# Modulation weights in hh and hl, small loads on GpSimd's queue, and an earlier place for casts of w_out, in a two-layer decoder trunk

## The chip, the cores and the metric

The kernel runs on one core of a Trainium2 chip. The metric is the device time of one execution in microseconds; several executions are timed and their median is given. One execution is also recorded by the hardware profiler; its rows are what the text reads.

## The reference

Two layers work on x of 512 positions by 1024 features, all in float32. Each layer has a token-mixing half and a feed-forward half, both modulated by a vector c:

```python
for l in range(DEPTH):                                     # 2
    mod = c_act @ ada_w[l] + ada_b[l]                      # 1024 -> 6 x 1024
    shift1, scale1, gate1, shift2, scale2, gate2 = jnp.split(mod, N_MOD, axis=-1)
    h = _modulate(x, shift1, scale1)                       # x * (1 + scale) + shift
    proj = jnp.einsum('bsd,de->bse', h, w_in[l])           # a | u | v, 3 x 512
    y_a = _pool_mixer(a, pool_w[l], pool_scale[l])         # trailing means, 4 groups
    y_b = _sgu_mixer(u, v, ...)                            # gelu(u) * (tril(W) Norm(gelu(v)) + b)
    f = jnp.einsum('bse,ed->bsd', jnp.concatenate([y_a, y_b], -1), w_out[l])
    x = _layernorm(DEEPNORM_ALPHA * x + gate1[:, None, :] * f, ln1_g[l], ln1_b[l])
    h = _modulate(x, shift2, scale2)
    g, val = split(jnp.einsum('bsd,df->bsf', h, w_up[l]))  # 2 x 2816
    f = jnp.einsum('bsf,fd->bsd', jax.nn.gelu(_causal_dwconv(g, ...)) * val, w_down[l])
    x = _layernorm(DEEPNORM_ALPHA * x + gate2[:, None, :] * f, ln2_g[l], ln2_b[l])
```

## The kernel before

Every weight comes from HBM in tiles of 128 x 1024 floats (512 KB), and each product is done in three parts: a weight is split into whi (a cast on ScalarE, L156) and wlo (a subtraction on VectorE, L159, the *low part*), an activation into hh and hl, mh and ml or gh and gl, and hi by hi, hi by lo and lo by hi are added on TensorE. Loads go through four raw tiles; split weights through six pairs.

The modulation (mod above) is not a product on TensorE: for each of the 6 x 8 pieces of a layer a 512 KB tile of ada_w is loaded and VectorE multiplies it with c and sums along the row (ada_sum, L206, a *modulation sum* of 128 x 1024). Tiles for these weights are three of their own (ada) and the four tiles xr, into which x itself is loaded later: when an xr tile has been summed and at least X_AT = 14 loads have been made, the next load into it is x (L213). For layer 0, pieces 1 and 0 (scale1, shift1) are summed first, two per step; then pieces 2, 4 and 3, 24 sums that pump() strews over the rest of the mixing half, in numbers that MIX_FILL and OUT_FILL fix. gate1 (piece 2) is needed by the first residual (L292), scale2 and shift2 (pieces 4, 3) by the modulation behind the norm.

Everything is written in one order, each engine works through its instructions in that order, and so does SP, which issues all loads. Layer 0 begins with a loop of eight steps k (L495): in each, two modulation sums give scale and shift for 128 features, ScalarE makes hh[k] and then x modulated in float32 (L475, L476), VectorE makes hl[k] (L479), and TensorE adds the products of step k to a and v (L527, L530), which lie in eight PSUM banks. Loads for step k + 2 are issued in step k. The order of w_in is in FIRST. Behind that loop SP loads what is small: pool_w, sgu_w and sgu_b (256 KB each), the counts of the trailing means (rcnt), columns of layer 1 (cols) and, as single floats, the gain and bias of the gating norm (sgc, sbc).

Then come u's four products (u_tile), the pooling on VectorE (pool_group), the norm of v, z (z_mms on TensorE, z_mix: two VectorE instructions per head, a cast mh on ScalarE, and ml on VectorE), the output projection by w_out: first half of the columns for all four chunks of 128 positions (project), then the second half chunk by chunk (project_and_norm). In the latter VectorE makes the residual and the norm of a chunk, and TensorE transposes it (tr_n, L302), one chunk behind its products. Each refill(1) splits one more weight: cast, low part, and a load that takes the raw tile which came free.

Of the kernel before, what the change touches and what calls it, by code (L numbers as in the profile page):

```python
# [29 lines left out]
X_AT = 14  # L30
# [9 lines left out]
def trunk(ctx: ExitStack, tc: tile.TileContext, a: dict, out: bass.AP):  # L40
# [6 lines left out]
    wsplit = ctx.enter_context(tc.tile_pool(name="wsplit", bufs=N_SPLIT))  # L47
    rows = ctx.enter_context(tc.tile_pool(name="rows", bufs=2))
# [23 lines left out]
    ada_free = araw + xr  # L72

    def load_ada(at):
        raw = ada_free.pop(0)
        nc.sync.dma_start(raw, a["ada_w"][at])
        return raw

# [118 lines left out]


# [16 lines left out]
    def ada_load(n):  # L215
        for _ in range(n):
            i = ada_at["load"]
            if i < len(ada):
                ada_raw.append(load_ada(ada[i]))
                ada_at["load"] += 1  # L220
# [10 lines left out]
    def pump(n=1, upto=None):  # L231

        for _ in range(n):
# [3 lines left out]
            ada_load(len(ada_free) - 1)  # L237
# [29 lines left out]
    hh = const.tile([P, KD, S], F32R, name="hh")  # L267
    hl = const.tile([P, KD, S], F32R, name="hl")
# [187 lines left out]
    def first_load(k):  # L456

        if k >= KD:
            ada_load(k - KD + 2)
# [4 lines left out]
        wload(len(FIRST[k]))  # L464
# [28 lines left out]
    first_lo(0)  # L493
    late.pop()()
    for k in range(KD):  # L495
# [10 lines left out]
        if k + 1 < KD:  # L506
            first_w(k + 1, late)
            first_h(k + 1, *firsts[k + 1])
            for f in late:
                f()  # L510
            late.clear()
            first_lo(k + 1)
# [37 lines left out]
    for l in range(L):  # L550
# [8 lines left out]
        poolw, wst, sb = [unit(f"{n}{l}") for n in ("poolw", "wst", "sb")]  # L559
        nc.sync.dma_start(poolw, a["pool_w"][l])  # L560
        nc.sync.dma_start(wst, a["sgu_w"][l])
        nc.sync.dma_start(sb, a["sgu_b"][l : l + 1, :].partition_broadcast(P))
        if l == 0:
            nc.sync.dma_start(rcnt, a["rcnt"])
            nc.sync.dma_start(cols[1], a["cols"][1])
            with nc.allow_non_contiguous_dma(reason="columns of the gating norm"):
                for t, n in ((sgc, "sgu_ln_g"), (sbc, "sgu_ln_b")):
                    for i in range(L):
                        nc.sync.dma_start(t[:, i, :], a[n][i].rearrange("(h d) -> d h", h=4))
# [137 lines left out]
        else:  # L707
# [22 lines left out]
            ps = u_tile(3)  # L730
            step(pms)
# [22 lines left out]
        ada_flush(True)  # L754
        AB = affine_cols(l, 1, col[:, C_G1 : C_G1 + 8], col[:, C_B1 : C_B1 + 8])
# [127 lines left out]
```

## Time and profile before

| what | value |
|---|---|
| median of 3 runs | 1022.68 us (1021.92 to 1022.88) |
| the profiled execution, time | 1023.64 us |
| the profiled execution, span | 1021.9 us |
| TensorE (PE) busy | 986.9 us, 97% |
| VectorE (DVE) busy | 650.2 us, 64% |
| ScalarE (ACT) busy | 364.0 us, 36% |

A busy share is a mean over the whole span. The change touches the first 140 us of it, where the engines are loaded otherwise than later; what waits there is read from timelines (instructions in order of time, with the idle time ahead of each and what ended it), from the sums of waits, and from windows that give the work of each engine in a stretch.

### The profile page before, as it was taken

The numbers are of one execution on the slowest core, as the hardware profiler recorded it, in microseconds if no ns is written. First come the engines' busy times: TensorE is split into PE (matmuls) and PEld (weight loads), VectorE is DVE, ScalarE is ACT, GpSimd is POOL, SyncE is SP. The second block draws the span as 40 slices with busy tenths as digits, with TensorE's granted clock in tenths as the row PEclk, the third lists the DMA queues.
The fourth block names the chain that finished last, engine by engine and source line by source line (L and its number), as shares of the span: only waits on it lengthen the run. The fifth ranks groups of instructions, "written<-read, shape, count | busy, mean of one in ns | idle before, by whom it ended". The sixth has DMA issues, their size and how long they took to land.

```text
span 1021.9 us, 12000 instructions
## 1 busy us (share of the span) xinstructions
PE 986.9 (97%) x4691; PEld 826.8 (81%) x4691; DVE 650.2 (64%) x907; ACT 364.0 (36%) x532; POOL 102.6 (10%) x80
## 2 busy tenths in 40 slices
PE   7999778999999999999999999999999999999996
PEld 6888568888888888888889878888888888888886
DVE  7878786878754276585599554877544245544456
ACT  4553254434322233333263432733433123333300
POOL 0020017200000000000045100450000000000002
PEclk9999999999999999999999999999999999999999
DMA  9985714666642355467114321345323322323302
GB/s 355 406 305 182 249 44 168 233 217 226 207 142 83 124 172 199 143 230 247 61 62 162 106 73 42 104 168 203 113 94 104 103 86 100 103 83 103 124 1 83
DMA packets 46233, 153.55 MB, mean 150 GB/s; under 512 B 7264, under 2 KB 7520, under 8 KB 46176
## 3 DMA queue, kind: packets, MB, share of 16 engines
q1 hardware_dynamic: 46176, 152.78, 43.7%
q8 instruction: 37, 0.61, 0.3%
q14 instruction: 20, 0.16, 0.0%
HBM read 150.67 MB, written 2.10 MB: 149 GB/s over the span
## 4 chain that ended last, share of the span: by engine, by line
PE 85%; DVE 9%; DMA 2%; ACT 1%; issue 1%; POOL 1%; SPq 0%; DVEq 0%; POOLq 0%; ACTq 0%
PE up L195 15%; PE up L196 15%; PE up L194 15%; PE down L342 6%; PE down L341 6%; PE down L340 6%; PE v L527 2%; PE u L196 1%; PE u L195 1%; PE u L194 1%; DVE wlo L159 1%; DVE res L292 1%; PE a L527 1%; DVE stn L381 1%; DMA ada<-in_ada_w_dram 1%
## 5 line engine op out<-in xcount | busy, mean ns | idle before, releaser
L196 PE MATMUL up<-hh,wlo 128*128 128x512 f32 (+1 forms) x768 | 286.1, 373 | 2.4 <-DVE wlo L159 2.4
L195 PE MATMUL up<-hl,whi 128*128 128x512 f32 (+1 forms) x768 | 286.0, 372 | 2.3 <-DVE hl L317 2.3
L194 PE MATMUL up<-hh,whi 128*128 128x512 f32 (+1 forms) x768 | 286.5, 373 | 0.0
L159 DVE TENSOR_TENSOR wlo<-raw_w_up,whi 128x1024 fp32r<-128x1024 f32 x88 | 119.0, 1357 | 143.4 <-ACT whi L156 143.4
L195 PEld LDWEIGHTS up<-hl,whi 128*128 128x128 f32 x768 | 145.4, 189 | 27.7 <-DVE hl L317 2.7
L196 PEld LDWEIGHTS up<-hh,wlo 128*128 128x128 f32 x768 | 145.3, 189 | 27.5 <-DVE wlo L159 2.8
L194 PEld LDWEIGHTS up<-hh,whi 128*128 128x128 f32 x768 | 145.4, 189 | 24.9
L159 DVE TENSOR_TENSOR wlo<-raw_w_down,whi 128x1024 fp32r<-128x1024 f32 x44 | 53.9, 1225 | 114.9 <-ACT whi L156 114.9
L156 ACT CAST whi<-raw_w_up 128x1024 fp32r<-128x1024 f32 x88 | 90.9, 1045 | 57.0 <-PE down L342 52.6
L340 PE MATMUL down<-whi,gh 128*128 128x512 f32 x272 | 105.8, 389 | 0.0
L341 PE MATMUL down<-wlo,gh 128*128 128x512 f32 x272 | 105.8, 389 | 0.0
L342 PE MATMUL down<-whi,gl 128*128 128x512 f32 x272 | 105.8, 389 | 0.0
L206 DVE SCALAR_TENSOR_TENSOR ada<-ada,c 128x1024 f32<-128x1024 f32 x80 | 97.2, 1219 | 8.7 <-DMA ada<-in_ada_w_dram 8.5
L777 ACT ACTIVATE y<-y 128x512 f32<-128x512 f32 x44 | 27.9, 634 | 143.2 <-DVE y L774 143.2
L156 ACT CAST whi<-raw_w_down 128x1024 fp32r<-128x1024 f32 x44 | 46.1, 1047 | 80.6 <-PE down L342 76.2
L767 ACT ACTIVATE y<-up,cols 128x512 f32<-128x512 f32 x44 | 34.3, 780 | 90.9 <-PE up L196 90.9
L341 PEld LDWEIGHTS down<-wlo,gh 128*128 128x128 f32 x272 | 51.1, 188 | 10.7
L340 PEld LDWEIGHTS down<-whi,gh 128*128 128x128 f32 x272 | 51.1, 188 | 10.6
L342 PEld LDWEIGHTS down<-whi,gl 128*128 128x128 f32 x272 | 51.0, 188 | 10.5
L314 ACT ACTIVATE ht_n<-tr_n,B,A 128x128 f32<-128x128 f32 x96 | 36.1, 455 | 64.5 <-PE tr_n L302 64.5
L275 POOL TENSOR_SCALAR rs_n<-mv_n 128x1 f32<-128x1 f32 x12 | 7.2, 600 | 490.6 <-DVE mv_n L273 490.6
L781 ACT CAST gh<-y 128x512 fp32r<-128x512 f32 x44 | 27.3, 621 | 43.7 <-DVE y L779 43.7
(159 smaller groups left out, 1449.4 us busy)
## 6 DMA issues: line engine op xcount, KB each, us to landing
raw_w_up<-in_w_up_dram SPq DMA_DIRECT2D x88, 512.0 KB, 3.3
ada<-in_ada_w_dram SPq DMA_DIRECT2D x80, 512.0 KB, 4.4
raw_w_down<-in_w_down_dram SPq DMA_DIRECT2D x44, 512.0 KB, 3.3
raw_w_in<-in_w_in_dram SPq DMA_DIRECT2D x24, 512.0 KB, 5.7
xr<-in_ada_w_dram SPq DMA_DIRECT2D x16, 512.0 KB, 9.2
raw_w_out<-in_w_out_dram SPq DMA_DIRECT2D x16, 512.0 KB, 4.2
xT<-in_xT_dram SPq DMA_DIRECT2D x8, 256.0 KB, 9.0
xr<-in_x_dram SPq DMA_DIRECT2D x4, 512.0 KB, 4.4
```

The costliest lines, as they stand in the source:

```text
L156: A.copy(hi, src)
L159: (eng or V).tensor_tensor(lo, src, hi.bitcast(F32), op=ALU.subtract)
L194: T.matmul(ps, w[0], x[0], start=start, stop=False)
L195: T.matmul(ps, w[0], x[1], start=False, stop=False)
L196: T.matmul(ps, w[1], x[0], start=False, stop=stop)
L206: V.scalar_tensor_tensor(raw, raw, 0.5, c2, op0=ALU.mult, op1=ALU.mult, accum_out=modc[l][:, o : o + 1])
L314: A.activation(tmp[:, w], ps[hf][:, w], AF.Identity, bias=cb[:, k : k + 1], scale=ca[:, k : k + 1])
L340: T.matmul(ps[:, f], ah[:, cs], wh, start=i + j == 0, stop=False)
L341: T.matmul(ps[:, f], ah[:, cs], wl, start=False, stop=False)
L342: T.matmul(ps[:, f], al[:, cs], wh, start=False, stop=i + j == n - 1)
L527: T.matmul(ps, x, y, start=k == 0 and i == 0, stop=False)
L767: A.activation(y, pg, AF.Identity, bias=col[:, C_CB + j : C_CB + j + 1], scale=col[:, cw + 2 : cw + 3])
```

## The change

- hh and hl are no longer fixed tiles. A pool of four tiles of 128 x 4 x 512 (tag h) holds them; a small class, Parts, gives slices by step as before. When u's last product is written, hand_over() issues all four loads of x into xr, and takes the four pool tiles as eight tiles for modulation weights (lent_h). After the first half of the output projection hh and hl are taken from the pool again.
- Two tiles of the rows of the norms (tag nrow), not yet in use, are lent to the modulation weights from the beginning (lent). Loads from the 12th of the list on (LENT = 11) take only tiles of their own until hand_over(); after it, loads up to the 24th take any.
- The small loads are issued on GpSimd's queue at the beginning.
- The first w_in load stands ahead of the second ada_w load; in step 0 the products of v come ahead of those of a.
- hl[k] is written on VectorE after the first modulation sum of the next step.
- The casts of the third and fourth w_out tile stand ahead of the z casts, with their low parts later, and two modulation sums stand ahead of the second w_out's low part.

```diff
-X_AT = 14
+LENT = 11
...
+    hpool = ctx.enter_context(tc.tile_pool(name="hpool", bufs=4))
...
-    ada_free = araw + xr
+    lent = xr + [rows.tile([P, D], F32, tag="nrow", name=f"lent{i}") for i in range(2)]
+    ada_free = araw + lent
...
+    class Parts:
+        def renew(self, name):
+            self.tiles = [hpool.tile([P, 4, S], F32R, tag="h", name=f"{name}{i}") for i in range(2)]
...
+    poolw, wst, sb = mix_loads(0, G)
+    G.dma_start(rcnt, a["rcnt"])
+    G.dma_start(cols[1], a["cols"][1])
+    with nc.allow_non_contiguous_dma(reason="columns of the gating norm"):
+        for t, n in ((sgc, "sgu_ln_g"), (sbc, "sgu_ln_b")):
+            for i in range(L):
+                G.dma_start(t[:, i, :], a[n][i].rearrange("(h d) -> d h", h=4))
...
-        c = next((c for c in range(NCH) if xr[c] is raw), None)
-        if c is None or ada_at["load"] < X_AT:
-            ada_free.append(raw)
-        else:
-            nc.sync.dma_start(raw, a["x"][c * P : (c + 1) * P, :])
+        ada_free.append(raw)
...
+            own = i >= (24 if mixed else LENT)
...
+    def hand_over():
+        for c in range(NCH):
+            nc.sync.dma_start(xr[c], a["x"][c * P : (c + 1) * P, :])
+        mixed.append(True)
+        ada_free[:] = [t for t in ada_free if among(t, araw)]
+        for i in range(4):
+            t = hpool.tile([P, 4, S], F32, tag="h", name=f"lent_h{i}").rearrange("p a b -> p (a b)")
+            ada_free.extend([t[:, :D], t[:, D:]])
...
-        raw = [load_ada((0, v, k)) for v in (1, 0)]
+        raw = [load_ada((0, 1, k))]
+        wload(k == 0)
+        raw.append(load_ada((0, 0, k)))
...
             ada_sum(0, 1 - v, k, raw[v])
+            if k and v == 0:
+                first_lo(k - 1)
...
+        if k == 0:
+            products = products[1:] + products[:1]
...
             ps = u_tile(3)
+            hand_over()
             step(pms)
             pump(MIX_FILL[2], fill)
             pms = step([pool_mix(2), pool_mix(3)])
             u_gelu(3, ps)
-            refill(1)
-            step(pms)
+            refill(1, None, late)
             z_mms()
             pump(MIX_FILL[3], fill)
+            late.pop()()
+            step(pms)
+            refill(1, None, late)
             zs = step([z_mix(0), z_mix(1)])
-            refill(1)
+            late.pop()()
             pump(MIX_FILL[4], fill)
             step(zs)
+            refill(1, None, late)
             zs = step([z_mix(2), z_mix(3)])
-            refill(1)
+            late.pop()()
...
+        if l == 0:
+            hh.renew("hh")
+            hl.renew("hl")
```

Where it moves instructions is seen best in the engines' own lists. On SP, at the start, before: ada_78 and ada_79 are modulation weights, raw_w_in the first two tiles of w_in.

```order
L76 DMA ada_78<-in_ada_w_dram 128x1024
L76 DMA ada_79<-in_ada_w_dram 128x1024
L463 DMA xT_158<-in_xT_dram 128x512
L66 DMA raw_w_in_160<-in_w_in_dram 128x1024
L66 DMA raw_w_in_162<-in_w_in_dram 128x1024
```

The same place now:

```order
L82 DMA ada_81<-in_ada_w_dram 128x1024
L67 DMA raw_w_in_176<-in_w_in_dram 128x1024
L82 DMA ada_82<-in_ada_w_dram 128x1024
L512 DMA xT_179<-in_xT_dram 128x512
L67 DMA raw_w_in_181<-in_w_in_dram 128x1024
```

The first tile of w_in moved from the fourth place to the second. Further down on SP, around the loads of x, before (raw_w_out are the tiles of w_out in their order):

```order
L213 DMA xr_81<-in_x_dram 128x1024
L66 DMA raw_w_out_642<-in_w_out_dram 128x1024
L66 DMA raw_w_out_690<-in_w_out_dram 128x1024
L66 DMA raw_w_out_764<-in_w_out_dram 128x1024
L213 DMA xr_82<-in_x_dram 128x1024
L213 DMA xr_83<-in_x_dram 128x1024
L66 DMA raw_w_out_813<-in_w_out_dram 128x1024
L213 DMA xr_84<-in_x_dram 128x1024
L66 DMA raw_w_out_856<-in_w_out_dram 128x1024
L76 DMA ada_80<-in_ada_w_dram 128x1024
L66 DMA raw_w_out_878<-in_w_out_dram 128x1024
L76 DMA ada_78<-in_ada_w_dram 128x1024
```

And now, from the third tile of w_out on:

```order
L67 DMA raw_w_out_769<-in_w_out_dram 128x1024
L264 DMA xr_84<-in_x_dram 128x1024
L264 DMA xr_85<-in_x_dram 128x1024
L264 DMA xr_86<-in_x_dram 128x1024
L264 DMA xr_87<-in_x_dram 128x1024
L82 DMA ada_83<-in_ada_w_dram 128x1024
L82 DMA lent_h_801<-in_ada_w_dram 128x1024 x2
...
L67 DMA raw_w_out_832<-in_w_out_dram 128x1024
L82 DMA lent_88<-in_ada_w_dram 128x1024
L82 DMA lent_89<-in_ada_w_dram 128x1024
L67 DMA raw_w_out_864<-in_w_out_dram 128x1024
```

The loads of x stand together, and eight loads into hh and hl (lent_h, of which two are shown) stand ahead of the fourth tile of w_out. On VectorE, behind the low parts of the first two poolings' outputs, before (L206 is a modulation sum, L159 a low part of w_out, L602 and L649 are ml, L637 and L645 z):

```order
L206 SCALAR_TENSOR_TENSOR xr_83,modc_146<-xr_83,c_102 128x1024
L159 TENSOR_TENSOR wlo_810<-raw_w_out_690,whi_809 128x1024
L602 SCALAR_TENSOR_TENSOR ml_801<-pm_798,psc_537,mh_800 128x512
L602 SCALAR_TENSOR_TENSOR ml_806<-pm_803,psc_537,mh_805 128x512
L206 SCALAR_TENSOR_TENSOR xr_84,modc_146<-xr_84,c_102 128x1024
L206 SCALAR_TENSOR_TENSOR ada_78,modc_146<-ada_78,c_102 128x1024
L637 SCALAR_TENSOR_TENSOR z_840<-z_817,sgc,zb_542 128x512
L645 TENSOR_TENSOR z_840<-z_840,u_610 128x512
L637 SCALAR_TENSOR_TENSOR z_846<-z_822,sgc,zb_542 128x512
L645 TENSOR_TENSOR z_846<-z_846,u_669 128x512
L159 TENSOR_TENSOR wlo_853<-raw_w_out_764,whi_852 128x1024
```

And now:

```order
L243 SCALAR_TENSOR_TENSOR lent_89,modc_155<-lent_89,c_111 128x1024
L243 SCALAR_TENSOR_TENSOR ada_81,modc_155<-ada_81,c_111 128x1024
L243 SCALAR_TENSOR_TENSOR ada_82,modc_155<-ada_82,c_111 128x1024
L181 TENSOR_TENSOR wlo_830<-raw_w_out_695,whi_829 128x1024
L646 SCALAR_TENSOR_TENSOR ml_821<-pm_818,psc_547,mh_820 128x512
L646 SCALAR_TENSOR_TENSOR ml_826<-pm_823,psc_547,mh_825 128x512
L681 SCALAR_TENSOR_TENSOR z_866<-z_834,sgc,zb_552 128x512
L689 TENSOR_TENSOR z_866<-z_866,u_619 128x512
L681 SCALAR_TENSOR_TENSOR z_872<-z_839,sgc,zb_552 128x512
L689 TENSOR_TENSOR z_872<-z_872,u_674 128x512
L181 TENSOR_TENSOR wlo_862<-raw_w_out_769,whi_861 128x1024
```

Two sums moved from behind the second w_out's low part to ahead of it; the rest stands as it did.

## Rows read from the trace of the kernel before

**Rows 1.** TensorE's timeline: start us, us, instruction, [idle before <- what ended it].
```profile
12.71 0.80 PE L527 MATMUL a<-hh,whi 128*128 128x512 f32 x1 [3.67 <-ACT whi L156]
24.50 0.39 PE L196 MATMUL a<-hh,wlo 128*128 128x512 f32 x1
84.72 1.88 PE L597 MATMUL pm<-ws,poolw 128*128 128x512 f32 x4
136.27 1.07 PE L302 MATMUL tr_n<-ident,xr 128*128 128x128 f32 x8 [3.62 <-DVE xr L387]
```

**Rows 2.** Waits in the first 200 us: who waits for whom, total us, times, longest.
```profile
PE n_pj L341 <- DVE wlo L159: 5.4, 2, 4.0
PE out L342 <- DVE ml L649: 1.2, 1, 1.2
PE out L341 <- DVE wlo L159: 0.5, 1, 0.5
DVE ada L206 <- DMA ada<-in_ada_w_dram: 8.5, 5, 4.1
```

**Rows 3.** VectorE's timeline, same columns as rows 1.
```profile
21.23 2.36 DVE L159 TENSOR_TENSOR wlo<-raw_w_in,whi 128x1024 fp32r<-128x1024 f32 x2
59.11 1.22 DVE L206 SCALAR_TENSOR_TENSOR ada<-ada,c 128x1024 f32<-128x1024 f32 x1 [4.13 <-DMA ada<-in_ada_w_dram]
69.58 1.23 DVE L159 TENSOR_TENSOR wlo<-raw_w_in,whi 128x1024 fp32r<-128x1024 f32 x1 [1.63 <-ACT whi L156]
84.45 1.22 DVE L206 SCALAR_TENSOR_TENSOR xr<-xr,c 128x1024 f32<-128x1024 f32 x1
85.59 1.22 DVE L206 SCALAR_TENSOR_TENSOR xr<-xr,c 128x1024 f32<-128x1024 f32 x1
88.77 1.23 DVE L159 TENSOR_TENSOR wlo<-raw_w_out,whi 128x1024 fp32r<-128x1024 f32 x1 [1.96 <-ACT whi L156]
93.52 0.75 DVE L637 SCALAR_TENSOR_TENSOR z<-z,sgc,zb 128x512 f32<-128x512 f32 x1
98.02 1.23 DVE L159 TENSOR_TENSOR wlo<-raw_w_out,whi 128x1024 fp32r<-128x1024 f32 x1 [1.64 <-ACT whi L156]
106.01 1.22 DVE L159 TENSOR_TENSOR wlo<-raw_w_out,whi 128x1024 fp32r<-128x1024 f32 x1 [1.63 <-ACT whi L156]
109.50 1.22 DVE L159 TENSOR_TENSOR wlo<-raw_w_out,whi 128x1024 fp32r<-128x1024 f32 x1
128.22 1.23 DVE L206 SCALAR_TENSOR_TENSOR ada<-ada,c 128x1024 f32<-128x1024 f32 x1 [1.30 <-DMA ada<-in_ada_w_dram]
130.13 0.68 DVE L292 TENSOR_TENSOR res<-out,gate 128x512 f32<-128x512 f32 x1
```

**Rows 4.** Windows: stretch, busy us by engine, granted clock, DMA share, GB/s last.
```profile
44.00:53.00 9.00, 9.00 (x41) 7.48 (x40) 8.48 (x21) 2.78 (x4) 0.00 (x0) 1.00 1.03 404
53.00:55.50 2.50, 2.50 (x12) 2.07 (x12) 1.98 (x4) 0.00 (x0) 0.64 (x1) 1.00 0.65 95
76.00:86.00 10.00, 10.00 (x43) 7.17 (x42) 9.76 (x21) 4.10 (x7) 0.00 (x0) 1.00 0.02 7
```

**Rows 5.** SP's timeline of issues: start us, us, line, loads in a row.
```profile
68.40 2.77 SPq L66 DMA_DIRECT2D raw_w_out<-in_w_out_dram  x3
85.70 1.47 SPq L213 DMA_DIRECT2D xr<-in_x_dram  x2
```

**Rows 6.** Loads by tile: count, KB each, median us from issue to landing.
```profile
raw_w_up<-in_w_up_dram SPq DMA_DIRECT2D x88, 512.0 KB, 3.3
poolw<-in_pool_w_dram SPq DMA_DIRECT2D x2, 256.0 KB, 6.9
```

**Rows 7.** ScalarE's timeline, same columns as rows 1.
```profile
10.07 0.81 ACT L475 ACTIVATE hh<-xT,B,A 128x512 fp32r<-128x512 f32 x1
20.69 1.05 ACT L156 CAST whi<-raw_w_in 128x1024 fp32r<-128x1024 f32 x1 [0.23 <-DMA raw_w_in<-in_w_in_dram]
87.70 1.04 ACT L156 CAST whi<-raw_w_out 128x1024 fp32r<-128x1024 f32 x1
```

More of the change, by code (lines that the diff above doesn't have):

```diff
@@ L71, in trunk, with among, load_ada, __getitem__ @@
     xr = [const.tile([P, D], F32, name=f"xr{c}") for c in range(NCH)]
-    ada_free = araw + xr
-    def load_ada(at):
-        raw = ada_free.pop(0)
+    lent = xr + [rows.tile([P, D], F32, tag="nrow", name=f"lent{i}") for i in range(2)]
+    ada_free = araw + lent
+    def among(t, ts):
+        return any(t is x for x in ts)
+    def load_ada(at, own=False):
+        raw = next(t for t in ada_free if not own or among(t, araw))
+        ada_free[:] = [t for t in ada_free if t is not raw]
         nc.sync.dma_start(raw, a["ada_w"][at])
         return raw
+    class Parts:
+        def renew(self, name):
+            self.tiles = [hpool.tile([P, 4, S], F32R, tag="h", name=f"{name}{i}") for i in range(2)]
+        def __getitem__(self, at):
+            _, k, t = at
+            if isinstance(k, slice):
+                return self.tiles[k.start // 4][:, :, t]
+            return self.tiles[k // 4][:, k % 4, t]
+    hh, hl = Parts(), Parts()
+    hh.renew("hh_0")
+    hl.renew("hl_0")
     c_in = const.tile([P, KD], F32, name="c_in")
@@ L196, in mm3, with mix_loads @@
         T.matmul(ps, w[1], x[0], start=False, stop=stop)
+    def mix_loads(l, eng):
+        tiles = [unit(f"{n}{l}") for n in ("poolw", "wst", "sb")]
+        eng.dma_start(tiles[0], a["pool_w"][l])
+        eng.dma_start(tiles[1], a["sgu_w"][l])
+        eng.dma_start(tiles[2], a["sgu_b"][l : l + 1, :].partition_broadcast(P))
+        return tiles
+    poolw, wst, sb = mix_loads(0, G)
[5 more added lines that the diff above has]
+                G.dma_start(t[:, i, :], a[n][i].rearrange("(h d) -> d h", h=4))
     ada = [(0, v) for v in (2, 4, 3, 5)] + [(1, v) for v in (1, 0, 2, 4, 3, 5)]
@@ L208, in ada_sum, with ada_load @@
         )
-        c = next((c for c in range(NCH) if xr[c] is raw), None)
-        if c is None or ada_at["load"] < X_AT:
-            ada_free.append(raw)
-        else:
-            nc.sync.dma_start(raw, a["x"][c * P : (c + 1) * P, :])
-    def ada_load(n):
-        for _ in range(n):
-            i = ada_at["load"]
-            if i < len(ada):
-                ada_raw.append(load_ada(ada[i]))
-                ada_at["load"] += 1
+        ada_free.append(raw)
+    def ada_load(keep=0, most=9):
+        for _ in range(most):
+            i = ada_at["load"]
+            own = i >= (24 if mixed else LENT)
+            if i >= len(ada) or sum(1 for t in ada_free if not own or among(t, araw)) <= keep:
+                return
+            ada_raw.append(load_ada(ada[i], own))
+            ada_at["load"] += 1
+    mixed = []
+    def hand_over():
[6 more added lines that the diff above has]
+            ada_free.extend([t[:, :D], t[:, D:]])
     def ada_flush(now=False):
@@ L236, in pump @@
                 return
-            ada_load(len(ada_free) - 1)
+            ada_load(1)
             l, v, n_ = ada[i]
@@ L265, in affine_cols @@
         return ca, cb
-    hh = const.tile([P, KD, S], F32R, name="hh")
-    hl = const.tile([P, KD, S], F32R, name="hl")
     def rstd_of(st, name):
@@ L458, in first_load @@
         if k >= KD:
-            ada_load(k - KD + 2)
+            ada_load(1, 4)
             return
-        raw = [load_ada((0, v, k)) for v in (1, 0)]
+        raw = [load_ada((0, 1, k))]
+        wload(k == 0)
+        raw.append(load_ada((0, 0, k)))
         x = unit(f"xT{k}")
         nc.sync.dma_start(x, a["xT"][k])
-        wload(len(FIRST[k]))
+        wload(len(FIRST[k]) - (k == 0))
         firsts.append((x, raw))
@@ L492, in trunk @@
     refill(1, None, late)
-    first_lo(0)
     late.pop()()
@@ L511, in trunk @@
             late.clear()
-            first_lo(k + 1)
+        else:
+            first_lo(k)
         for ps, w in zip(a_ps[old:], a_w[old:]):
@@ L558, in trunk @@
             next_residuals(grow2, brow2)
[L559 to L569, printed above, removed]
+        if l:
+            poolw, wst, sb = mix_loads(l, nc.sync)
         at = []
```

## The prediction

> **What bounds the kernel now.** Read first where TensorE stands still [rows 1, 2]: it is the busy engine of this kernel, so a change pays where it waits. That is in three places: ahead of its first product (12.71 us), between 106 and 136 us (the three groups of waits for w_out's low parts and for ml in rows 2, and 3.62 us ahead of the first transposition, at 136.27), and for a little after that. Everything in the second place names VectorE. So the next view is VectorE's timeline [rows 3]: from 84 to 130 us it is almost full, and at its end stands the step that matters, the first residual at 130.13, which needs the gate and comes behind the 24 modulation sums of this layer in VectorE's order. From there to the transposition that TensorE waits for are 6.14 us (130.13 to 136.27), a chain of VectorE and GpSimd. So the end of this stretch is set by when VectorE gets through its list, and the question is how much of the list's time is waiting. Rows 2 and 3 tell: 1.96, 1.64 and 1.63 us for ScalarE's casts of w_out at 88.77, 98.02 and 106.01, and 8.5 us in five waits for modulation weights from HBM; the longest, 4.13 us, ends at 59.11, and the other four, 4.4 us, come late, the last at 128.22. The last view is the DMA's: in 76 to 86 us it moves 7 GB/s, while a full stretch moves 404 [rows 4]. The reason is SP's queue [rows 5]: after the third w_out load, at 71 us, its next entry, a load of x into an xr tile, waits until 85.70 for VectorE to have summed what is in that tile, and all weights stand behind it.
>
> **Edit 1: the tiles and SP's order.** Two tiles more (nine for seven) hold modulation weights, and when u is done eight more lie in hh and hl. SP's order puts all four loads of x and one of modulation weights right behind the third w_out load, then the eight lent loads, which wait for TensorE's last products of u. Those end at 84.72 [rows 1], and a load takes 3.3 us to land [rows 6], so the lent loads land from about 88 us on at 1.30 us each (512 KB at 404 GB/s), the eighth by 98. Behind them stand the fourth w_out load (99 to 100) and the last two of the 24 sums' loads (102 to 103). The new wait on SP is thus the one for u, with everything down to w_up queued behind it; the queue stands empty meanwhile, as it did before. Who needs it: the sums 15 to 24, the first at about 102 us and the last at 118 (below), so the margin is over 10 us; the fourth w_out, cast at about 100 and wanted by VectorE at 100.6, which is the tight one, at most a few tenths; and w_out five to eight, landed by about 110 and wanted from 104 to 116. The four DMA waits of 4.4 us go.
>
> **Edit 2: casts ahead of z's, two sums earlier.** On ScalarE the third w_out cast moves ahead of the first two z casts, the fourth ahead of the next two; none waits for z any more, and ScalarE has time there (the second cast is at 87.70 [rows 7], the first z at 93.52). On VectorE two sums move ahead of the second w_out's low part, into the 1.96 us wait. I walk the new list with the pitch of rows 3: a sum 1.14 us (84.45 to 85.59), a low part the same (its row, as the sum's, says 1.22, of which 0.08 overlap the next), a z 1.4 (two from 93.52 to 96.38, where the wait of 1.64 begins), a pair of ml 1.2 to 1.3. The start is 84.45 as before: up to 69.58 VectorE now runs ahead of ScalarE, but there it waits for a cast that stands behind ScalarE's norm and gelu, whose order is unchanged, and from 69.58 to 84.45 it is full either way. So what VectorE saves before 69.58 (the 4.13 us wait among it) is **not** gained. From 84.45: four sums to 89.0, low part to 90.2, two ml to 91.5, two z to 94.3, low part 95.4, sum 96.6, two ml 97.8, two z 100.6, low part 101.7, sum 102.9, two ml 104.1; then four low parts, nine sums and the columns of the affine, 4.6 + 10.3 + 0.8, to 119.8. Before it was 130.13: **10.3 us less**. From below: the waits named are 1.96 + 1.64 + 1.63 + 4.4 = 9.6; from above, the list without any gap, 10.6.
>
> Is VectorE still the last one then? TensorE was done with the second chunk's products at 136.27 - 3.62 = 132.65; less its waits for low parts and ml, 0.5 + 1.2 + 5.4 [rows 2], it would be by 125.5; the transposition's data come at 119.8 + 6.1 = 125.9. They are nearly equal, so more than 0.4 us beyond this could not be had on VectorE alone. Behind that point the orders of all engines are the same in both kernels, and so are the waits up to the first up-projection (SP's loads of the norm's rows behind w_up, ScalarE behind those): they move with it. hh and hl are taken again after the last sum that reads a lent tile, which is over by then: no wait.
>
> **Edit 3: the start.** The first w_in load moves one place up, and the first products use it alone (v ahead of a): they need its cast and hh, which ends at 10.07 + 0.81 = 10.9 [rows 7], so TensorE starts up to 1.8 us before 12.71. But this is not kept. The third step's weights are the next fence: the cast at 20.69 waits for their landing [rows 7], the two low parts run from 21.23 to 23.6 [rows 3], and TensorE takes the second at 24.50 [rows 1]. So at most 0.9 us is gained. hl one sum later costs nothing: VectorE gives up waits of half a us for ScalarE there, and TensorE reads hl only at the end of each step.
>
> **Edit 4: small loads on GpSimd's queue.** They leave SP's queue and now run at the very start. Price: three loads of 256 KB [rows 6] and 0.1 MB besides, 0.89 MB at 404 GB/s, 2.2 us; and four loads of single floats (512 pieces each): in 53 to 55.5 us [rows 4], where they ran before, the DMA was busy 0.65 of 2.5 us, 1.6, while its 0.24 MB are worth 0.6, so 1.0 us. In the first 50 us HBM's stream is the fence, so landings come 2.2 to 3.2 us later: the cast of the third step ends at 21.7 + 2.2 to 3.2, its low part 1.14 later, 25.0 to 26.0 against 24.50, a loss of 0.5 to 1.5 us. Later steps have more slack (TensorE does 8 groups a step by then), so it stays at that. No row shows a DMA from GpSimd, so the term lies between a gain of 0.9 (they come later than the third step) and 1.5 lost; I take **0.8 lost**, since the stretch at 404 GB/s leaves nothing free. TensorE, ScalarE's norms and so VectorE's 69.58 all move with it. The Trainium skill, page "DMA: Bandwidth & Descriptors", section "Queues, rings and completion order", says that a DMA engine takes turns between the rings that have work, packet by packet; no run here shows it with a GpSimd queue, and it would put the small loads into the first 10 us rather than behind SP's stream.
>
> **Sum.** -10.3 + 0.8 = -9.5. The profiled execution took 1023.64 us (span 1021.9), 1 us over the median; it would become 1014.1, and the median of 1022.68 becomes **1013.2**. The bounds: 1022.68 - 10.6 - 0.9 = 1011.2 to 1022.68 - 9.6 + 1.5 = 1014.6.
>
> **Rivals.**
> (a) The small loads come late and the start's 0.9 us is kept: 1022.68 - 10.3 - 0.9 = 1011.5. For it: GpSimd has to make these transfers itself, one after the other, 2,048 pieces of single floats among them. VectorE's first use of any (the counts) comes behind the sum of 59.11, so lateness costs nothing. 17%. The Trainium skill, page "SBUF — State Buffer", section "SBUF: two separate sides", has a rule that would do this: while VectorE holds the port that it shares with GpSimd, GpSimd cannot write its descriptors; no trace here shows a case of it.
> (b) The small loads weigh more, by up to 1.4 us, because the two streams also hold up the second step: 1014.6 to 1016. 12%.
> (c) The lent loads still come late for the sums, since they wait for u and stand eight deep ahead of w_out: the 4.4 us stay, 1013.2 + 4.4 = 1017.6. Against it is the margin of 10 us. 6%.
> (d) **Slower**: the single floats on GpSimd's queue at the start. They cost 1.0 us for 2,048 now. The start has 0.9 us of slack and the change gains 10.3 us, so the kernel gets slower by over 2 us once the small loads cost 0.9 + 10.3 + 2 = 13.2 us, which is 11 us for the floats, eleven times the price of now. 3%.
> (e) The order doesn't do what it says, VectorE waits elsewhere as long: 1022.7. Against it is the walk, which has room at each point but one. 2%.
>
> **Chances.** The forecast has 60%. The range of 1010.7 to 1016 takes in the forecast's bounds, (a) and (b), with half a us for the spread of runs below; (c), (d) and (e) are left out. Faster by over 0.2% (about what a measurement of this kernel can tell from no change): 60 + 17 + 12 + 6 = 95%; within: 2%; slower: 3%.
>
> **What would show it.** In the profile after: no wait of VectorE for a modulation load after 60 us; its waits for casts of w_out from the second on gone; the first residual at about 120.6 (119.8 and the 0.8) and the first transposition at about 126.7, with TensorE waiting little for low parts of w_out; DMA near 0 GB/s before u ends, and full behind it. At the start: the first product at 11 to 12 us, the low part of the third step's second weights later than 24.50. Wrong would be: a wait for the lent loads, or TensorE idle for several us in the first 30 us.

## The result and the profile after

The changed kernel takes 1016.87 us (1016.08 to 1017.41), the kernel before beside it 1022.75: a ratio of 0.9944 (95% interval 0.9926 to 0.9961), 5.9 us less. A second series of both gave 0.9932 (0.9919 to 0.9944). The forecast was 1013.2 with a range of 1010.7 to 1016.0: the direction is right, the time 3.7 us too low, 0.9 us outside the range. The profiled execution took 1017.41 us, its span is 1015.7 (before: 1021.9).

VectorE's timeline between the first of the four sums and the first residual, against [rows 3] (sums are L243 now, low parts L181, z L681, the residual L339):

```profile
87.43 1.22 DVE L243 SCALAR_TENSOR_TENSOR lent<-lent,c 128x1024 f32<-128x1024 f32 x1
...
92.01 1.22 DVE L181 TENSOR_TENSOR wlo<-raw_w_out,whi 128x1024 fp32r<-128x1024 f32 x1
...
94.46 0.74 DVE L681 SCALAR_TENSOR_TENSOR z<-z,sgc,zb 128x512 f32<-128x512 f32 x1
...
104.63 1.22 DVE L243 SCALAR_TENSOR_TENSOR lent_h<-lent_h,c 128x1024 f32<-128x1024 f32 x1
...
120.89 1.22 DVE L243 SCALAR_TENSOR_TENSOR lent<-lent,c 128x1024 f32<-128x1024 f32 x1
122.80 0.68 DVE L339 TENSOR_TENSOR res<-out,gate 128x512 f32<-128x512 f32 x1
```

No row has a wait in brackets: the list runs through. From 87.43 to 122.80 are 35.37 us, where 84.45 to 130.13 were 45.68 [rows 3]: **10.31 us less**. TensorE's waits around it, against [rows 1, 2]:

```profile
119.88 0.50 PE L388 MATMUL n_pj<-wlo,mh 128*128 128x512 f32 x1 [0.56 <-DVE wlo L181]
128.94 1.07 PE L349 MATMUL tr_n<-ident,xr 128*128 128x128 f32 x8 [2.19 <-DVE xr L434]
```

Of 5.4 us for low parts of w_out 0.56 are left, and the first transposition stands at 128.94 instead of 136.27, 7.33 us earlier. The other 2.98 of the 10.31 were lost before: the first sum stood at 84.45 and now stands at 87.43. So the start has to be read. Here are ScalarE's first casts and hh, then TensorE's first product and its take-up of the third step's second low part (L218), against [rows 1, 7]:

```profile
8.16 1.05 ACT L178 CAST whi<-raw_w_in 128x1024 fp32r<-128x1024 f32 x1 [3.49 <-DMA raw_w_in<-in_w_in_dram]
13.41 0.81 ACT L526 ACTIVATE hh<-xT,B,A 128x512 fp32r<-128x512 f32 x1 [4.20 <-DMA xT<-in_xT_dram]
25.04 1.05 ACT L178 CAST whi<-raw_w_in 128x1024 fp32r<-128x1024 f32 x1 [0.23 <-DMA raw_w_in<-in_w_in_dram]
```

```profile
14.28 0.79 PE L580 MATMUL v<-whi,hh 128*128 128x512 f32 x1 [5.22 <-ACT hh L526]
27.40 0.50 PE L218 MATMUL a<-hh,wlo 128*128 128x512 f32 x1 [0.53 <-DVE wlo L181]
```

The first weight is cast a microsecond earlier than before, but hh waits for xT until 13.41 (10.07 before), the third step's cast comes at 25.04 (20.69), and TensorE takes its low part at 27.40 (24.50): 2.9 us late. Windows of the changed kernel (DMA share and GB/s last) and its DMA queues over the first 30 us (packets, MB, share of 16 engines' time; q0 is GpSimd's):

```profile
6.00:10.00 4.00, 3.06 (x15) 2.87 (x14) 1.23 (x2) 1.05 (x1) 2.06 (x3) 1.00 0.98 328
10.00:14.00 4.00, 0.00 (x0) 0.00 (x0) 2.57 (x5) 0.59 (x1) 0.00 (x0) 1.00 1.08 289
14.00:18.00 4.00, 3.72 (x9) 2.95 (x10) 1.96 (x2) 1.97 (x3) 0.00 (x0) 1.00 1.04 409
q0 software_dynamic: 448, 0.89, 10.3%
```

From 6 to 14 us the DMA engines are fully busy and yet move 328 and 289 GB/s, not 404 as in [rows 4]. The small loads' packets took 10.3% of 30 us, 3.1 us, for 0.89 MB, which are worth 2.2 us at 404 GB/s. The cast came later than that, by 4.35 us (three more profiles of this kernel, below, have it at 25.14, 24.58 and 25.71 us); the experiments take it apart.

### The profile page after: what moved, and what is told of

Its sections match the earlier page's. It is cut to its first block, busy times and chain, and to the rows that moved or that the text cites. A ratio compares the mean times of both kernels' runs of the same rounds, so it can differ in the third digit from the quotient of the medians.

```text
span 1015.7 us, 11993 instructions
## 1 busy us (share of the span) xinstructions
PE 986.6 (97%) x4691; PEld 826.9 (81%) x4691; DVE 648.1 (64%) x907; ACT 364.1 (36%) x532; POOL 108.5 (11%) x89
## 4 chain that ended last, share of the span: by engine, by line
PE 83%; DVE 9%; DMA 3%; ACT 3%; issue 1%; POOL 1%; SPq 0%; DVEq 0%; POOLq 0%; ACTq 0%
PE up L217 15%; PE up L218 15%; PE up L216 15%; PE down L387 6%; PE down L388 6%; PE down L389 6%; DVE wlo L181 2%; PE n_pj L388 1%; PE n_pj L389 1%; PE n_pj L387 1%; DMA ada<-in_ada_w_dram 1%; PE v L580 1%; PE a L580 1%; DMA raw_w_in<-in_w_in_dram 1%; ACT ht_n L361 1%
## 5 line engine op out<-in xcount | busy, mean ns | idle before, releaser
L218 PE MATMUL up<-hh,wlo 128*128 128x512 f32 (+1 forms) x768 | 285.9, 372 | 2.4 <-DVE wlo L181 2.4
L181 DVE TENSOR_TENSOR wlo<-raw_w_up,whi 128x1024 fp32r<-128x1024 f32 x88 | 118.7, 1353 | 143.8 <-ACT whi L178 143.8
L218 PEld LDWEIGHTS up<-hh,wlo 128*128 128x128 f32 x768 | 145.2, 189 | 27.7 <-DVE wlo L181 2.8
L181 DVE TENSOR_TENSOR wlo<-raw_w_down,whi 128x1024 fp32r<-128x1024 f32 x44 | 53.9, 1225 | 114.9 <-ACT whi L178 113.3
L243 DVE SCALAR_TENSOR_TENSOR ada<-ada,c 128x1024 f32<-128x1024 f32 x68 | 82.6, 1217 | 4.4 <-DMA ada<-in_ada_w_dram 4.4
L181 DVE TENSOR_TENSOR wlo<-raw_w_in,whi 128x1024 fp32r<-128x1024 f32 (+1 forms) x26 | 37.8, 1477 | 10.0 <-ACT whi L178 9.9
```

The source lines that it names most:

```text
L181: (eng or V).tensor_tensor(lo, src, hi.bitcast(F32), op=ALU.subtract)
L218: T.matmul(ps, w[1], x[0], start=False, stop=stop)
L243: V.scalar_tensor_tensor(raw, raw, 0.5, c2, op0=ALU.mult, op1=ALU.mult, accum_out=modc[l][:, o : o + 1])
```

## The experiments

Theory 1: the late start is the small loads alone. The rivals put it on the new order of the first loads, or on another place. In all of them the same row is read, ScalarE's second cast of the third step.

**The small loads alone, taken away, and delayed.** The first kernel is the one before plus edit 4; the other three are the changed one:

```diff
 # b_small: the kernel before, and
+    poolw, wst, sb = mix_loads(0, G)      # and rcnt, cols[1], sgc, sbc on G, at the start
 # a_sp: the changed kernel, and
-    poolw, wst, sb = mix_loads(0, G)
+        else:                             # l == 0, behind the first loop
+            poolw, wst, sb = mix_loads(0, nc.sync)
 # a_hold: all of them; a_holdf: the four single-float loads only
+        if k == 4:
+            G.tensor_scalar(hold, B0[:, k : k + 1], 1.0, None, op0=ALU.add)
+            poolw, wst, sb = mix_loads(0, G)
```

> The kernel before, with nothing changed but the small loads, which go to GpSimd's queue at the beginning. Theory 1 (the small loads alone make the late start): the third step's second low part is taken by TensorE about 2.9 us later than 24.50, at about 27.4, all that follows moves by it, and the time is 1022.7 + 3.0 = 1025.7 us. Rival A (the price put on record, 0.5 to 1.5 us for them; the rest of the late start comes from the new order of the first loads and of hl): 1023.2 to 1024.2. Rival B (the late start has nothing to do with the small loads): 1022.7.

> The changed kernel, with the small loads back on SP's queue, behind the loop of eight steps as in the kernel before. Theory 1: the start is no later than in the kernel before (second low part of the third step at 23.6 to 24.5), so 3.0 to 3.9 us less than the changed kernel: 1013.0 to 1013.9 if TensorE's half-clock stretch of layer 1 (about 1.3 us) stays, 1011.7 to 1012.6 without it. Rival A: 1015.4 to 1016.4. Rival B (the new order of the first loads makes the start late): 1016.9.

> The changed kernel, with all small loads still on GpSimd's queue, but behind a one-column operation of GpSimd that reads step 4's shift, so that they start at about 30 us instead of 1.5 us. Theory 1: the early steps have no slack for 0.89 MB and the single floats, the later ones do (TensorE has eight groups of products a step by then): as with the small loads on SP, 1011.7 to 1013.9. Rival C (GpSimd's queue itself costs, whenever it runs beside a full stream of SP's): TensorE waits for a later step's weights instead by 2 to 4 us, and the time is 1015 to 1018.

> The changed kernel, with the four loads of single floats alone held until step 4; the five others start at the beginning as they do now. Theory 1 with the split read from the trace (of the 4.15 us by which SP's stream is behind at 14 us, 2.15 are the bytes of the small loads and 2.0 are lost beside the single floats): the third step's second low part is taken at about 25.4 instead of 27.4, 2.0 us less than the changed kernel, 1014.9. Rival D (the single floats cost what they did on SP's queue, 1.0 us): 1015.9. Rival E (the 0.89 MB are nothing and the single floats everything): 1012.5 to 1014.

| kernel | median us | ratio to before (95%) | second cast, third step |
|---|---|---|---|
| before plus edit 4 | 1028.75 | 1.0055 (1.0039 to 1.0070) | 25.09 |
| changed, small loads on SP | 1013.01 | 0.9895 (0.9879 to 0.9910) | 21.10 |
| changed, all held to step 4 | 1013.35 | 0.9896 (0.9883 to 0.9910) | 21.06 |
| changed, floats held | 1015.86 | 0.9922 (0.9910 to 0.9935) | 24.10 |

Here is TensorE's first product with edit 4 alone, and below it the take-up of the third step's low part in the changed kernel with the small loads on SP:

```profile
16.79 0.79 PE L542 MATMUL a<-hh,whi 128*128 128x512 f32 x1 [7.73 <-ACT whi L156]
```

```profile
23.82 0.50 PE L218 MATMUL a<-hh,wlo 128*128 128x512 f32 x1 [0.29 <-DVE wlo L181]
```

Theory 1 holds. Edit 4 alone makes the kernel before **slower**: its first product comes at 16.79 instead of 12.71, 4.1 us late. My 3.0 us were too few there: in the kernel before TensorE runs from its first product to 24.50 with one wait, 0.46 us ahead of the second product, so nothing is absorbed. The ratio gives 4.0 to 7.2 us, and the start's 4.1 lie within that. In the two profiles the distance is 4.2 us at TensorE's first wait for a low part of w_out (107.29 and 111.46), 4.6 at the first residual, 4.9 at 660 us, where TensorE waits 0.35 us longer for a transposition, and 5.1 at the end. Without the small loads at the start the changed kernel takes that low part at 23.82, against 27.40 with them: **3.6 us**. The new order of the first loads is thus innocent. Held to step 4, the same loads on the same queue cost nothing: two windows of that kernel show the same sag, at full share,

```profile
38.00:40.00 2.00, 2.00 (x10) 1.65 (x10) 1.33 (x4) 0.00 (x0) 1.39 (x2) 1.00 1.04 373
40.00:42.00 2.00, 2.00 (x11) 1.65 (x10) 1.24 (x4) 0.00 (x0) 0.00 (x0) 1.00 1.05 228
```

and TensorE is busy through both. The single floats are not the main part: holding them gains 0.9 us, the rival's 1.0, not the 2.0 that I had then read from the windows.

**Which of the small loads?** Two stay at the beginning, alone or with one or two others; the rest is held to step 4. In the last kernel sgu_b lies in HBM as 128 equal rows (for both layers; the times are read at the start, in layer 0).

```diff
 # a_two
+    G.dma_start(poolw, a["pool_w"][0])
+    G.dma_start(wst, a["sgu_w"][0])
 # a_pieces: as well
+    G.dma_start(rcnt, a["rcnt"])
+    G.dma_start(cols[1], a["cols"][1])
 # a_spread: a_two, and
+    G.dma_start(sb, a["sgu_b"][0:1, :].partition_broadcast(P))
 # a_rows: a_two, and
+    G.dma_start(sb, a["sgu_b"][0])        # laid out as 128 x 512
```

> The changed kernel with only pool_w and sgu_w (two loads of 256 KB, rows of 2 KB) at the beginning on GpSimd's queue; sgu_b (256 KB, spread to 128 partitions), the counts, the columns of layer 1 and the single floats are held until step 4. With everything but the single floats at the beginning the third step's second cast stood at 24.10 us, with all of them held at 21.10. Theory B (bytes count, whatever their form): 0.52 of 0.88 MB make 1.8 of the 3.0 us, cast at 22.9, and the time 1.2 us under the run with all but the single floats. Theory P (two loads of plain rows cost only what their bytes cost at 404 GB/s, and the rest is the spread load and the small pieces): 1.3 us, cast at 22.4. Theory N (any traffic of GpSimd's queue in the first 10 us costs about the same, by its rows being taken in turn with SP's): cast at 23.5 to 24.1.

> The changed kernel with pool_w, sgu_w, the counts and the columns of layer 1 at the beginning on GpSimd's queue, sgu_b and the single floats held until step 4. Theory S: cast at 22.3 to 22.5 (0.09 MB more than with pool_w and sgu_w alone, 22.14). Theory P: cast at 23.2 to 23.5.

> The changed kernel with pool_w, sgu_w and sgu_b at the beginning on GpSimd's queue, the counts, the columns of layer 1 and the single floats held until step 4. The third step's second cast stood at 22.14 us with pool_w and sgu_w alone and at 24.10 with the counts and columns too; 1.96 us for 0.36 MB, of which bytes explain 0.9. Theory S (sgu_b, one row of 2 KB that is read 128 times, costs more than its bytes): cast at 23.7 to 24.1. Theory P (its 256 KB cost 0.65 us as any other, and the rows of 64 and 704 bytes of counts and columns the rest): cast at 22.7 to 22.9, time about 0.6 us over the run with two loads.

> As the run with pool_w, sgu_w and sgu_b at the beginning on GpSimd's queue (third step's second cast at 23.68 us, against 22.14 without sgu_b), but sgu_b lies in HBM as 128 equal rows of 2 KB, so that the load is 256 KB of plain rows. In the run before, 8 to 10 us moved 203 GB/s at a busy share of 0.94. Theory F (the form costs: one row read 128 times over this queue): cast at 22.6 to 22.8, no such window, and 0.9 us less time. Theory Q (a third load of this queue costs that, whatever its form, because it is taken in turn with SP's loads): cast at 23.4 to 23.9 and the window stays.

| at the start on GpSimd's queue | median us | ratio to before (95%) | cast | step, us | bytes at 404 GB/s, us |
|---|---|---|---|---|---|
| nothing (small loads on SP) | 1013.01 | 0.9895 | 21.10 | | |
| pool_w, sgu_w | 1013.98 | 0.9905 (0.9891 to 0.9920) | 22.14 | 1.04 | 1.3 |
| these, counts, columns | 1014.61 | 0.9916 (0.9902 to 0.9930) | 22.48 | 0.34 | 0.24 |
| pool_w, sgu_w, sgu_b spread | 1015.64 | 0.9928 (0.9913 to 0.9943) | 23.68 | 1.54 | 0.65 |
| pool_w, sgu_w, sgu_b as rows | 1014.99 | 0.9917 (0.9900 to 0.9933) | 22.73 | 0.59 | 0.65 |
| all but the floats | 1015.86 | 0.9922 (0.9910 to 0.9935) | 24.10 | | |

(The steps of the middle rows are against 22.14.) Plain rows cost what their bytes cost or less; the load that spreads one row over 128 partitions cost 1.54 us, more than twice its bytes. Windows from 8 to 10 us, spread, and below it as plain rows:

```profile
8.00:10.00 2.00, 1.26 (x6) 1.08 (x6) 0.00 (x0) 1.04 (x1) 0.00 (x0) 1.00 0.94 203
```

```profile
8.00:10.00 2.00, 1.07 (x6) 0.88 (x5) 0.00 (x0) 1.04 (x1) 0.00 (x0) 1.00 1.03 401
```

and GpSimd's queue over the first 16 us, without sgu_b, with it spread, and with it as rows:

```profile
q0 software_dynamic: 160, 0.52, 8.1%
```

```profile
q0 software_dynamic: 240, 0.79, 17.7%
```

```profile
q0 software_dynamic: 240, 0.79, 12.2%
```

The same 80 packets and 0.26 MB took 9.6% of 16 us (1.54 us) spread and 4.1% (0.66 us) as rows. The row of the cast and the queue's row thus give the same price, and the form is its cause. The kernel with the floats held, which has the spread load as well, moves 222 GB/s from 8 to 10 us at a share of 0.95. The parts add up: 1.04 + 0.34 + 1.54 = 2.92, measured 3.00 for all but the floats, and 0.94 for the floats. Each step is a difference of single profiles. With the small loads on SP three profiles have the cast at 20.98 to 21.16, but the changed kernel's four have it at 24.58 to 25.71, so the floats' 0.94 may be 0.5 to 1.6; the medians, 1015.86 against 1016.87 and 1016.84, say 1.0.

**The halves of the 10.3 us.** From the kernel with the small loads on SP edit 2, and then edit 3, is taken back (as in the diff of the change, reversed); to the kernel before edit 2 alone is added.

> The kernel with the small loads back on SP's queue, and without edit 2: the casts of w_out behind z's and the two sums behind the second low part, as in the kernel before. The tiles lent for modulation weights and the new start stay. Theory 1 (the two halves of the 10.3 us add up: 4.4 us of waits for modulation loads by edit 1, 5.2 to 5.9 us by edit 2): three waits of VectorE for casts of 1.6 to 2.0 us are back, and the time is 5.2 to 5.9 us more than with edit 2, 1018.0 to 1018.9. Rival A (edit 1 does it all, VectorE's waits for casts fill with sums whose loads are now there): within 1 us of 1013. Rival B (without edit 2 the loads are late again, since the casts free the raw tiles that SP's queue waits for): 1020 to 1023.

> The kernel before with edit 2 alone: the casts of the third and fourth w_out ahead of z's, two sums ahead of the second low part. Tiles, loads and start as before. Theory 1 (edit 2 takes 5.3 us of waits for casts, edit 1 the 4.4 to 5 us of waits for loads, and they add up): 1022.7 - 5.3 = 1017.4, with the waits for modulation loads still there. Rival (loads bind: SP's queue still waits at 85.7 us for a sum, and what is cast earlier only makes VectorE wait longer for loads): a gain of 0 to 2 us, 1020.7 to 1022.7, with the waits for modulation loads and w_out longer by 3 to 5 us. Both can hold in part: then the gain of edit 1 given edit 2 is the larger one.

> The kernel with the small loads back on SP's queue, and without edit 3: the first loads, the order of the first products and the place of hl as in the kernel before. Theory 1 (edit 3 gains what TensorE's take-up of the third step's second low part shows, 24.50 against 23.81 us): 0.7 us more, 1013.7. Rival A (it gains the whole 1.5 us of the earlier first product, 12.71 against 11.18): 1014.5. Rival B (nothing is kept, since VectorE is full from 69.58 us on and starts there when ScalarE's norm lets it): 1013.0.

| kernel | median us | ratio to before (95%) | first sum to first residual |
|---|---|---|---|
| before | | 1 | 84.45 to 130.13: 45.68 |
| edit 2 alone | 1017.87 | 0.9944 (0.9931 to 0.9957) | 84.59 to 123.87: 39.28 |
| edits 1 and 3 | 1018.86 | 0.9949 (0.9936 to 0.9961) | 83.57 to 124.51: 40.94 |
| edits 1, 2 and 3 | 1013.01 | 0.9895 (0.9879 to 0.9910) | 83.84 to 119.22: 35.38 |
| edits 1 and 2 | 1015.10 | 0.9909 (0.9893 to 0.9924) | 85.08 to 120.44: 35.36 |

VectorE's waits with edit 2 alone, and below it with edits 1 and 3, over 60 to 136 us (the first includes the 4.1 us ahead of a sum that begins at 58.91):

```profile
DVE ada L206 <- DMA ada<-in_ada_w_dram: 7.7, 4, 4.1
```

```profile
DVE wlo L181 <- ACT whi L178: 5.6, 3, 2.0
DVE wlo L181 <- DMA lent<-in_ada_w_dram: 1.6, 1, 1.6
```

Each edit takes its own kind of wait: edit 2 alone leaves 3.6 us of waits for modulation loads, edits 1 and 3 leave those for casts. (The profile puts one of these, ahead of 97.21, down to the load of a lent tile; the cast of that weight, 96.13 to 97.18, ends just ahead of it, so I count it as one for a cast.) The gains are 6.40 and 4.74 us, 0.8 us more than the two together give. Edit 3 shows 1.4 us in the pair of ratios and in TensorE's row (25.21 to 23.82), against 0.7 from the kernel before (24.50 to 23.82). The median without edit 3, 1015.10, lies above all three expectations. Without edit 3 the first cast stood at 9.55 us here and at 9.12 before; kernels that begin alike (small loads on SP or held) have it anywhere from 6.97 to 7.61. So edit 3 is worth 0.7 to 1.4 us.

**TensorE's clock.** With the start as measured the changed kernel should be 10.3 - 2.9 = 7.4 us faster, and it is 5.9. The waits ahead of the transpositions of layer 1 are the same before and after, but the distance between the kernels is not: the first transpositions stand at 522.99 and 648.88 now,

```profile
522.99 1.85 PE L349 MATMUL tr_n<-ident,xr 128*128 128x128 f32 x8 [2.19 <-DVE xr L434]
648.88 1.47 PE L349 MATMUL tr_n<-ident,xr 128*128 128x128 f32 x8 [2.42 <-DVE xr L434]
```

and at 530.68 and 655.28 before: 7.69 us apart, then 6.40. Windows show why (granted clock third from the end); first the kernel before, then the changed one:

```profile
123.00:128.00 5.00, 3.65 (x10) 2.90 (x11) 2.52 (x5) 0.00 (x0) 0.00 (x0) 0.66 0.85 324
530.00:535.00 5.00, 4.32 (x37) 4.32 (x38) 4.84 (x3) 3.56 (x10) 4.92 (x3) 1.00 0.17 65
```

```profile
128.00:132.00 4.00, 3.06 (x18) 2.70 (x19) 3.93 (x7) 2.36 (x6) 0.00 (x0) 1.00 0.00 0
522.00:527.00 5.00, 4.01 (x21) 4.01 (x22) 4.48 (x3) 2.94 (x8) 4.92 (x3) 0.66 0.23 87
```

The engine waits 2.2 us ahead of the first transposition of a norm, and a stretch of some 3.4 us at half clock (0.50, so 1.2 instead of 2.4 GHz) may follow. The profile before has one at 124 us, the profile after at 523; both have one at about 650. The one at 124 came behind another wait, the longest for a low part of w_out, which the change takes away:

```profile
124.35 0.80 PE L341 MATMUL n_pj<-wlo,mh 128*128 128x512 f32 x1 [3.97 <-DVE wlo L159]
```

TensorE was through these products 3.62 us before it could begin the first transposition [rows 1], so this stretch cost the end nothing. That the kernels are 7.33 us apart at that transposition and 7.69 at 523 is not the clock either: they are 7.35 apart at the third transposition (152.41 and 159.76) and 7.68 behind the wait for hl that follows, first before, then now:

```profile
167.92 0.39 PE L195 MATMUL up<-hl,whi 128*128 128x256 f32 x1 [1.20 <-DVE hl L317]
160.24 0.39 PE L217 MATMUL up<-hl,whi 128*128 128x256 f32 x1 [0.66 <-DVE hl L364]
```

This wait differs between profiles of one kernel as well (0.84, 1.01 and 1.18 us with the small loads on SP). Is the place of the stretches the kernel's doing? Five more profiles, one with a second series, of the changed kernel and of that with the small loads on SP, both unchanged:

> The changed kernel itself, a second time, on the chip and beside the runs that the three others have. Question: does TensorE's half-clock stretch behind the first transposition of layer 1 (near 523 us, 1.3 us lost) stand in every execution? Theory 1: which of the three first transpositions (near 129, 523 and 649 us; each waits about 2.2 us) are followed by such a stretch changes from one execution to the next, so that about 1.3 us of the distance of 5.0 us between this kernel and the one with the small loads on SP's queue is no property of either: 1016.5 to 1017.5 for the median, in this profile the stretch at 129 or 649 or both. Rival (this kernel always has it at 523, since its phases stand otherwise): the same stretch at 523 again, and none at 129.

> The changed kernel, a third profile. In the two so far TensorE's half-clock stretch of some 3.5 us stands at 523 and 649 us in one, at 161 and 649 in the other, in neither behind the first transposition at 129, where it would cost about 0.3 us (waits for low parts behind it are shorter by the rest) instead of 1.2 to 1.5. Theory 1 (chance): some profile of this kernel has it at 129. Rival (a property of this kernel's phases): none has.

> The kernel with the small loads back on SP's queue, a second profile. In the first the stretches stand at 125 and 644 us. Theory 1 (chance): some profile of it has one at 157 to 163 or at 520 and is 1.0 to 1.5 us longer, about 1014.2. Rival: 125 and 644 again.

> The changed kernel, a fourth profile; theories as for the third.

> The kernel with the small loads back on SP's queue, a third profile; theories as for the second.

| profile | time, us | half-clock stretches begin at, us |
|---|---|---|
| changed, first | 1017.41 | 523, 649 |
| changed, second (series: median 1016.84) | 1017.58 | 161, 649 |
| changed, third | 1017.99 | 128, 524, 650 |
| changed, fourth | 1017.39 | 130, 649 |
| small loads on SP, first | 1012.87 | 125, 644 |
| small loads on SP, second | 1013.83 | 520, 646 |
| small loads on SP, third | 1013.56 | 520, 646 |

(All have one more from 1006 us or later, close to their end; the one at 161 follows waits of 0.88 and 0.64 us for hh and hl.) Theory 1 of these runs holds: the place changes from one execution to the next in both kernels. Not shown is that the change leaves the odds as they were. Of the eighteen profiles of this case, the three of kernels without edit 1 (before, edit 4 alone, edit 2 alone) have no stretch between 500 and 540 us and one at 120 to 128; nine of the fifteen with edit 1 have one at 520 to 525. Three are too few to tell. What one costs is read from the kernel with the small loads on SP, first profile, then second (L218 is the first up-projection's take-up of a low part):

```profile
125.35 1.69 PE L342 MATMUL tr_n<-ident,xr 128*128 128x128 f32 x8 [2.18 <-DVE xr L427]
141.64 0.38 PE L218 MATMUL up<-hh,wlo 128*128 128x256 f32 x1 [0.70 <-DVE wlo L181]
519.82 1.09 PE L342 MATMUL tr_n<-ident,xr 128*128 128x128 f32 x8 [2.21 <-DVE xr L427]
644.42 1.96 PE L342 MATMUL tr_n<-ident,xr 128*128 128x128 f32 x8 [2.43 <-DVE xr L427]
```

```profile
125.21 1.07 PE L342 MATMUL tr_n<-ident,xr 128*128 128x128 f32 x8 [2.14 <-DVE xr L427]
141.23 0.39 PE L218 MATMUL up<-hh,wlo 128*128 128x256 f32 x1 [1.67 <-DVE wlo L181]
519.68 1.16 PE L342 MATMUL tr_n<-ident,xr 128*128 128x128 f32 x8 [2.19 <-DVE xr L427]
645.49 1.09 PE L342 MATMUL tr_n<-ident,xr 128*128 128x128 f32 x8 [2.42 <-DVE xr L427]
```

At 125 us it costs 0.27 us by 141.64 (0.14 apart ahead of it, 0.41 behind it), since the wait for a low part that comes next is 0.97 shorter, and nothing by 519.82, where the two are 0.14 apart again; at 520 it costs 1.2 (124.60 against 125.81 to the next one). Profiles with the same places compare cleanly: small loads on SP, second, has a span of 1012.1, the changed kernel, first, 1015.7. The 3.6 us between them are the start's (27.40 against 23.69 us at the third step's low part, 3.7). Without edit 3 the stretches stand at 521 and 647, and the span is 1013.4, 1.3 more than the second's. The Trainium skill, page "TensorE: Matmul & The Clock Gate", section "Part 1: The HAM clock gate", says that the chip's watch on TensorE's activity runs freely and is not tied to the kernel's start; seven profiles in which the place changes agree.

## Why the prediction was right or wrong, step by step

- **What bounds the kernel, and edits 1 and 2: right, to the tenth.** The walk gave 35.4 us from the first sum to the first residual, the trace has 35.37, and no wait of VectorE for a modulation load or for a cast of w_out behind the first is left. SP issues the lent loads at 85.00, when u ends, and the sums come to them at 104.63; rivals (c), lent loads that come late, and (e), waits elsewhere, fell. Edits 1 and 2 alone give 4.7 and 6.4 us. One sign was misread: the DMA was to stand near 0 before u ends, and moves 287 GB/s in 76 to 86 us, because the loads of x now come there; nothing hung on it.
- **Edit 3: right by the row it was read from.** At most 0.9 us was to be kept, of 1.8 at the first product. That row moved by 0.7 (24.50 to 23.82). Taken back, edit 3 costs 1.3 to 1.5, above the bound; 0.4 of that is the later landing of the first weight in that profile.
- **Edit 4: the step that failed, by its size.** The mechanism was the one named: HBM's stream is the fence at the start, the small loads push the third step's cast, and that cast sets the end; the formula, cast and 1.14 us of low part, gives 25.04 + 1.05 + 1.14 = 27.23 for the measured 27.40. But the landings were to come 2.2 to 3.2 us later, and came 3.9 to 4.4 later (against the small loads on SP and against the kernel before): 1.0 for plain rows (I had 1.3), 0.3 for counts and columns (0.2), 0.9 to 1.0 for the floats (1.0), and **1.5 for the spread load of sgu_b, which I had at its bytes, 0.65**. The rest is within what executions differ by. Then I took 0.8 of the 0.5 to 1.5, on the lower side. So the term, which was edit 3's slack and edit 4's price together, came out at +2.9 instead of +0.8, and 2.1 of the 3.7 us stem from it. Two signs named ahead show it: the first product was to come at 11 to 12 us and came at 14.28, after TensorE had stood idle for 5.22 us, and the first residual was to stand at about 120.6 and stood at 122.80.
- Could the trace before have told? In part. There the same load is issued at 47 us and lands 8.4 later, at 55.4: within the 53 to 55.5 us of [rows 4] whose excess of 1.0 us I put down to the single floats alone.

```profile
L562 SPq DMA_DIRECT2D sb<-in_sgu_b_dram x1: 328/328/328, 47.0 to 47.0; - x1
DMA to landing us min/median/max: 8.4/8.4/8.4
```

- **Rivals.** (a), late small loads, is refuted: GpSimd issued the first at 1.50 and was through its list by 7.5 us; it is also what the kernel with held loads makes true, and the 1011.5 us given for it compare with 1013. (b), small loads that weigh more because the second step is held up too, is the nearest, 1014.6 to 1016, and still too low by 0.9. The second step is held up (its cast at 19.24 us instead of 14.89), but what sets the end is the third step's own landing. (d), a price of 11 us for the floats, is refuted: 0.9. Yet edit 4 by itself does make the kernel before slower, by 4.0 to 7.2 us.
- **Clock.** The sum took TensorE's clock to be the same before and after. The stretch at 523 us in the profile after cost 1.3 us (7.69 to 6.40), the one at 124 in that of before nothing: this is most of the other 1.6 us. Its place changes between executions of one kernel, so for a single pair of profiles it is luck; whether the change makes it likelier is open. The range had no room for it.

Of the 6.2 us between the two spans (the medians are 5.9 apart) that is: -10.3 for edits 1 and 2, -0.7 for edit 3, +3.6 for edit 4, -0.3 for the shorter wait for hl, +1.3 for the clock, and +0.2 unexplained.

## What to carry to other kernels

A load is not hidden by moving it to another queue: at the start, where the DMA is already full (390 GB/s from 6 to 10 us and 414 from 10 to 14 in the kernel before), 0.89 MB ahead of the first weights cost 3.6 us, and the same loads 30 us later nothing. Price a transfer by its form and not only by its bytes, and look for a stretch of full DMA share and low GB/s; the load that spreads one row over all partitions was the dearest of the small ones. The version with the small loads back on SP's queue, 1013.0 us, beats both kernels; the one with sgu_b as plain rows in HBM shows that the form can be mended too.

## What the runs showed that was not expected

- One row of 2 KB, read for 128 partitions over GpSimd's queue, took 1.54 us of 16 DMA engines, the same 256 KB as 128 rows 0.66 us. Whether it is as dear on SP's queue is open: layer 1's, which is there in every kernel, landed 4.8 to 6.7 us after issue spread and 4.5 as rows, beside other traffic.
- The floats' own packets take nearly nothing: GpSimd's queue had 10.1% of the first 30 us without them and 10.3% with them, 0.06 us, while the cast moved by 0.94. They slow SP's stream. SP's queue (q1) over the first 16 us with the floats held, and below it with them:

```profile
q1 hardware_dynamic: 1450, 3.85, 66.4%
```

```profile
q1 hardware_dynamic: 1295, 3.48, 66.4%
```

  that is 10% fewer bytes in the same time of the engines (three more profiles with them: 3.53 to 3.58 MB in 67.3 to 69.0%). How, no run here shows.
- Plain rows of GpSimd's queue pushed SP's stream by no more than their own bytes (1.04 and 0.59 us for 1.3 and 0.65), and landed 5.0 to 7.7 us after issue, although SP had its loads queued all that time. That agrees with the turns between rings of the Trainium skill, page "DMA: Bandwidth & Descriptors", section "Queues, rings and completion order", cited ahead.
